# A hybrid attention block on Trainium2: the turned halves of a head are joined first in a period, its product moves between the second and the third projection quarter, and gates and norm rows are turned without TensorE

## The chip, the cores and the metric

The kernel runs on one core of one Trainium2 chip. Its time is the device time of one execution in microseconds (us); lower is better. The program has one instruction list for each engine: TensorE (PE in the profile, with weight loads as PEld), VectorE (DVE), ScalarE (ACT), GpSimd (POOL), and SyncE (SP), which here issues the DMA transfers. An engine works through its list in order, so an instruction that waits holds back everything listed behind it on that engine.

## The reference

One layer of a hybrid block for 512 tokens of width 2048, in float32. A combined projection gives queries, keys and values for eight "stick-breaking" heads (called sb below) and eight "forgetting" heads (called fox), each 128 wide, and eight forget gates.

```python
h = rmsnorm(x, g_attn[l])
proj = jnp.einsum('bsd,de->bse', h, w_in[l])
...
# sb head: strictly causal
log_beta = jax.nn.log_sigmoid(z)
log_keep = jnp.where(causal, jax.nn.log_sigmoid(-z), 0.0)
rest = lax.cumsum(log_keep, axis=3, reverse=True) - log_keep
a = jnp.where(causal, jnp.exp(log_beta + rest), 0.0)      # o = a @ v
# fox head: causal softmax with a bias from the summed log gates
z = z + c[:, :, i * Q_BLOCK:end, None] - c[:, :, None, :end]
p = jax.nn.softmax(jnp.where(causal, z, -jnp.inf), axis=-1)   # o = p @ v
...
x = x + jnp.einsum('bse,ed->bsd', mixed, w_out[l])   # mixed: each head's o, normalised
u = jax.nn.relu(jnp.einsum('bsd,df->bsf', rmsnorm(x, g_mlp[l]), w_up[l]))
x = x + jnp.einsum('bsf,fd->bsd', u * u, w_down[l])
```

The result is `rmsnorm(x, g_final)`.

## The kernel before

Every product is made with operands split into a high and a low part, both in a 32-bit format that TensorE reads in one pass; three matmuls (high by high, high by low, low by high) stand for one. The split of a weight tile costs ACT a cast (`cast`, tile `wh`) and DVE a subtraction (`low`, tile `wl`).

The program has stages: the first value projections, the projection of all other values with a seven-product scheme, the attention stage, and then the output, up and down projections, again with seven-product schemes. The change lies in the attention stage and just ahead of it.

The attention stage is cut into periods, numbered n = 0 to 16, each planned for 26.05 us (`TPER`). Jobs are entered with a planned time (`plan.at`), and the planned times only set the order in which instructions are recorded: each engine's list follows them, and no instruction waits for its planned time. In period n:

- PE projects the queries and keys of head n in four quarters (`project`, 24 matmuls each, tile `accq`): query first half, query second half, key first half, key second half. Between the first and the second quarter stand the scores of head n-1 (`scores`, tile `s`), and later the product of head n-2 with its values (`product`, tile `o`) and two matmuls that sum the squares of that product over the head (`norm_sums`, tile `ssq`).
- ACT and DVE turn the scores of head n-1 into weights in tile `w`. For a fox head these are `start`, `maxed`, `soft`, `scale`; for an sb head `start` (absolute value, ACT), `soft` (exponential and logarithm, ACT), `maxed` (DVE), `scan` (four running sums and a subtraction, DVE) and `weights` (exponential, ACT). Heads 0 to 7 of the order are fox, 8 to 15 sb, so scores are fox in n = 1 to 8 and sb from n = 9 on.
- The weights must be transposed. ACT copies them into two planes of 16-bit halves (`halves`, tile `pt`), a DMA transposes both planes (`turn_halves`), and in the next period ACT joins the halves again (`join_halves`, tile `pt`), casts the high part (`t_high`, tile `ph`), and DVE makes the low part (`t_low`, tile `pl`). `product` needs both.
- After the product, `square` (three ACT instructions), `square_low` (DVE; its result is what the second `norm_sums` matmul reads), `norm_1` (ACT) and `norm_2` (DVE) normalise the head.
- Beside this, the output weights are prepared by `WeightSums`: `high` and `low` split a part (tile `tboth`) that is stored to `wraws`, `sum` forms differences that are stored to `wsums`, `high_6` and `low_6` split one of these (tile `thi`) and store it to `whigh`. `tboth` and `thi` share one buffer, so each of these casts waits until the store of the one before has landed. In the fox periods the weights come in whole rows (`whole`, tile `mixed`): `high` stands once in every period and `high_6` in odd ones. Later they come in halves of a row (`half`, tile `ws`): in periods 8, 10, 12 and 14 stand both `high` and `high_6`, in periods 9, 11, 13 and 15 the `sum` steps alone.

Two more things belong to the change. The logs of the forget gates are summed with small matmuls into `cps` (`gates_3`), turned with four TensorE transposes (`gates_5`), and stored as `ckd` for the fox heads. And the row norms `r1`, which stand one per partition, are needed along the columns: `widen_r1` and `turn_r1` spread and turn them with four TensorE transposes into `trb`, and ACT copies them to `rb`, which `scale_u` multiplies into every query and key.

Up to period 2 the order of SP is the written one too; after it (`free_loads`) the tool that builds the program orders SP's transfers.

Of the kernel before, what the change touches and what calls it, by code (L numbers as in the profile page):

```python
# [8 lines left out]
F32 = mybir.dt.float32  # L9
# [6 lines left out]
P = 128  # L16
# [21 lines left out]
def block_kernel(ctx, tc, x, g_attn, w_in, b_f, g_out_sb, g_out_fox, w_out, g_mlp, w_up, w_down, g_final, y):  # L38
# [82 lines left out]
    vd = [dp.tile([P, TB, 2 * P], F32, name="vd0")] + [dp.tile([P, TB, 2 * NV], F32, name=f"vd{i}") for i in (1, 2)]  # L121
    ckd = dp.tile([NH, NT], F32, name="ckd")
    whigh = dp.tile([P, NH // 2, 2, NT], F32, name="whigh")

# [92 lines left out]
    with ExitStack() as stage:  # L217
# [352 lines left out]
        def gates_0():  # L570
            t_ = vf.tile([P, K8 * 2 * P], F32, tag="e3", name="gt")
            gate["tri"], gate["one"] = t_[:, :P], t_[:, P:2 * P]
            r_ = vf.tile([P, K8 * 2 * P], F32R, tag="e4", name="gr")
            gate["utri"] = r_[:, :P]
            gate["lf"] = r_[:, P:P + TB * 2 * NH].rearrange("p (t n) -> p t n", t=TB)
            gate["fe"] = t_[:, 4 * P:4 * P + TB * NH].rearrange("p (t n) -> p t n", t=TB)
            gate["ckT"] = t_[:NH, 5 * P:5 * P + NT]
# [19 lines left out]
        def gates_3():  # L597
            ps = gate["ps"] = accs[0].tile([P, NT], F32, tag="acc", name="cps")
            cps = gate["cps"] = ps[:, :TB * 2 * NH].rearrange("p (t n) -> p t n", t=TB)
            for t in range(TB):  # L600
                for i in range(t + 1):
                    pe.matmul(cps[:, t, :], gate["utri"] if i == t else onesr, gate["lf"][:, i, :], start=(t == 0 and i == 0),
                              stop=(i == t), skip_group_check=True)

# [4 lines left out]
        def gates_5():  # L609
            for t in range(TB):  # L610
                pe.transpose(gate["ps"][:NH, t * P:(t + 1) * P], cq[:, t, :], ident)
# [94 lines left out]
    with tc.tile_pool(name="att", bufs=1, side="right", reuse_waits="tile") as at, \  # L706
# [15 lines left out]

        def widen_r1():
            w = now["rw"] = at.tile([P, NT], F32, tag="uh4", name="rw")
            for t in range(TB):
                dve.tensor_copy(w[:, t * P:(t + 1) * P], r1[:, t:t + 1].to_broadcast([P, P]))

        def turn_r1():
            now["rb"] = atp.tile([P, NT], F32, tag="o", name="trb")
            for t in range(TB):  # L730
                pe.transpose(now["rb"][:, t * P:(t + 1) * P], now["rw"][:, t * P:(t + 1) * P], ident)

# [54 lines left out]
        class Head:  # L787
# [13 lines left out]
            def plan_sb(self, plan, t):  # L801
# [24 lines left out]
                last_ = self.i == 2 * NH - 1  # L826
                for dt, f in zip((6.4, 7.7, 10.2, 14.5, 19.2) if last_ else (7.4, 8.7, 11.25, 16.45, 21.1), (start, soft, maxed, scan, weights)):
                    plan.at(t + dt, f)

            def plan_fox(self, plan, t):  # L830
# [27 lines left out]

                for dt, f in zip((-4.0, 7.4, 12.2, 15.5, 17.8), (load, start, maxed, soft, scale)):
                    plan.at(t + dt, f)  # L860
# [13 lines left out]
            def turn_halves(self):  # L874
                self.two = wide("ph")
                sp.dma_start_transpose(self.two.bitcast(U16).rearrange("p (b t) -> p b t", t=P), self.one.bitcast(U16))
# [114 lines left out]
        def whole(m, t):  # L991
            w = WeightSums(m, (0, 1), lambda: mixed[:, :NH].rearrange("p (q a) n -> p q (a n)", a=2))
            e, o = (t, t + TPER) if m else (TPER, TPER)
            loads = (-4.0 if m == 1 else -15.0, 2.7) if m else (20.5, 20.6)
            highs, lows_, sums_, sixth = ((e + 3.0, o + 3.0), (e + 4.75, o + 4.75), (e + 5.5, e + 16.4, o + 5.5, o + 16.4), (o + 10.2, o + 20.2)) if m else \
                ((e + 4.3, e + 10.0), (e + 4.75, e + 10.9), (e + 5.5, e + 14.9, e + 19.6, e + 20.9), (e + 21.5, e + 23.3))
            for i in range(2):
                plan.at(t + loads[i], w.load, (i,))
                plan.at(highs[i], w.high, i)
                plan.at(lows_[i], w.low, i)  # L1000
            for i in range(4):
                plan.at(sums_[i], w.sum, i)
            plan.at(sums_[1] + 0.1, lambda: w.store(0, 2))
            plan.at(sixth[0], w.high_6)
            plan.at(sixth[1], w.low_6)
            plan.at(sixth[1] + 0.1, lambda: w.store(2, 4))

        def half(m, d, n):
# [8 lines left out]
            if d == 0:  # L1017
                jobs = [(8.3 if n == 7 else 13.0, load if n == 7 else w.load)]
                a = (3.0, 4.75, 5.5, 6.2, 6.9, 10.2, 16.4, 17.1, 20.8, 22.9) if n == 7 else (4.85, 6.2, 8.3, 9.0, 9.7, 11.15, 12.75, 13.45, 16.6, 23.2)
                jobs += [(TPER + dt, f) for dt, f in zip(a, (lambda: w.high(0), lambda: w.low(0), lambda: w.sum(0), lambda: w.sum(1), lambda: w.sum(2),  # L1020
                                                             lambda: w.high(1), lambda: w.low(1), lambda: w.sum(3), w.high_6, w.low_6))]
                jobs += [(TPER + a[-1] + 0.1, w.store)]
            else:
                jobs = [(TPER + 3.0, w.load)]
                jobs += [(TPER + dt, lambda j=j: w.sum(j)) for j, dt in enumerate((9.5, 10.2, 12.75, 13.45))] + [(TPER + 13.55, w.store)]
            for dt, f in jobs:
# [23 lines left out]
        for n in range(2 * NH + 1):  # L1050
            t = TPER * n
            i_s, i_o = n - 1, n - 2
            if n < 2 * NH:
                pieces = []
                for a, (which, hf) in enumerate(((0, 0), (0, 1), (1, 0), (1, 1))):
# [9 lines left out]
                    else:  # L1065
                        cast, low = ((-8.15, -4.45), (2.0, 3.5), (5.6, 9.4), (9.0, 10.6))[a] if n <= NH else ((-11.15, -3.55), (2.0, 3.5), (3.7, 4.9), (6.0, 7.1))[a]
                        if a == 0 and n == NH + 1:
                            cast, low = -8.15, -4.45
# [6 lines left out]
                late = n <= NH  # L1075
                for which, times in ((0, (19.0, 19.75, 20.45) if n == 0 else (14.2, 14.95, 19.5) if late else (14.2, 16.0, 21.8)),
                                     (1, (TPER + 0.3, TPER + 1.05, TPER + 2.6))):
                    for dt, f in zip(times, (scale_u, high_u, low_u)):
                        plan.at(t + dt, f, n, which)
            else:  # L1080
                pieces = []
                for a in range(4):
                    c = v_columns(order[2 * NH - 2])
                    k0 = 4 * a
                    w = Piece(w_in[k0 * P:(k0 + 4) * P, c:c + 2 * P].rearrange("(a p) c -> p a c", p=P), 4, 2 * P)
                    cast, low = ((-11.15, -3.55), (2.0, 3.5), (3.7, 4.9), (10.25, 11.7))[a]
                    pieces.append(w.plan(plan, t + (-21.0, -15.0, -14.0, -2.0)[a], t + cast, t + low))
# [8 lines left out]
            if 0 <= i_s < 2 * NH:  # L1096
# [4 lines left out]
                if n < 2 * NH:  # L1101
                    plan.at(t + (25.2 if sb else 23.8), H.halves)
                    plan.at(t + 26.2, H.turn_halves)
                else:
# [4 lines left out]
                if i_s % 2 == 0 and i_s < 2 * NH - 2:  # L1109
                    p_ = i_s // 2  # L1110
                    plan.at(t - 12.0 if p_ else t + 3.0, load_v, p_)
                    plan.at(t + (4.85 if sb else 6.7 if p_ else 12.0), high_v, p_)
                    plan.at(t + (8.3 if sb else 23.0 if p_ else 16.4), low_v, p_)
            if 0 <= i_o < 2 * NH - 1:
                H = heads[i_o]
                last_ = i_o == 2 * NH - 2
                for dt, f in zip((11.25, 13.6, 19.3) if last_ else (11.2, 13.7, 14.9), (H.join_halves, H.t_high, H.t_low)):
                    plan.at(t + dt, f)
                if last_:
                    continue  # L1120
                plan.at(t + 16.5, H.product)
                plan.at(t + 18.5, H.square)
                plan.at(t + 21.1, H.square_low)
                plan.at(t + 22.3, H.norm_sums)
                plan.at(t + 22.5, H.norm_1)
                plan.at(t + (24.4 if n > NH else 23.9), H.norm_2)
        for i, dt in ((2 * NH - 2, 1.0), (2 * NH - 1, 3.0)):
# [6 lines left out]
            plan.at(t_end + dt + 6.3, H.norm_2)  # L1134
        for dt, f in ((16.25, widen_r1), (17.0, turn_r1), (17.5, lambda: act.copy(rb, now["rb"]))):
            plan.at(dt, f)
        for m in range(4):
# [970 lines left out]
```

## Time and profile before

| | us |
|---|---|
| median of 3 runs | 2030.81 (2030.69 to 2032.73) |
| the profiled execution's own time | 2030.32 |
| its span, first to last instruction | 2028.6 |
| PE busy | 2004.1 (99%) |
| DVE busy | 1740.5 (86%) |
| ACT busy | 1204.0 (59%) |

The profiled execution's time is its span and 1.7 us around it. PE is busy in nearly all of the span, and a granted clock of 0.998 stands for the whole. Rows of the timeline give the start in us from the span's start, the duration, the engine, the line, the operation and the tiles; in brackets stands the idle time of that engine before the row and what ended it. Period n of the attention stage begins 5.45 us ahead of its scores, since a quarter of the projection takes that long.

### The profile page before, as it was taken

Reading aid. Unit: us, or ns where it says so; the run is one execution under the profiler, and the core shown is the slowest. Engines: PE = TensorE matmul, PEld = TensorE weight load, DVE = VectorE, ACT = ScalarE, POOL = GpSimd, SP = SyncE. Lnnn points to the kernel's source line nnn. Section 1 sums busy time; section 2 is a strip of 40 time slices with the busy share of each in tenths; the row PEclk is TensorE's granted clock in tenths of the full one; section 3 lists DMA queues with packets and bytes.
Section 4 is the critical chain, followed back from the end, with each engine's and each line's share of the span. In section 5 each row is a group of like instructions: output and inputs, shape, how many; then the busy total and the mean of one; then the engine's idle time right before and its main releaser. Section 6 shows DMA issues by size and latency. Waiting matters only on the chain.

```text
span 2028.6 us, 27079 instructions
## 1 busy us (share of the span) xinstructions
PE 2004.1 (99%) x10316; PEld 1733.7 (85%) x10316; DVE 1740.5 (86%) x1971; ACT 1204.0 (59%) x1645; POOL 60.3 (3%) x72
## 2 busy tenths in 40 slices
PE   9999999999999999999999999999999999999998
PEld 9998888877788889988888888888888888888887
DVE  7876787777778588899999999998799888888896
ACT  7544666777775556666767677676544343444444
POOL 0000000001010000000000000000000000000003
PEclk9999999999999999999999999999999999999999
DMA  7418877766667982576666666667785674674642
GB/s 261 154 63 263 263 221 214 225 186 194 182 211 261 298 272 86 161 242 188 208 210 184 217 202 195 208 194 252 249 299 198 224 261 166 233 259 170 223 159 89
DMA packets 309074, 423.28 MB, mean 209 GB/s; under 512 B 49176, under 2 KB 204872, under 8 KB 302416
## 3 DMA queue, kind: packets, MB, share of 16 engines
q1 hardware_dynamic: 308192, 419.44, 63.6%
q10 hardware_dynamic: 752, 2.11, 0.3%
q8 instruction: 81, 1.33, 0.3%
q14 instruction: 49, 0.40, 0.1%
HBM read 315.19 MB, written 96.49 MB: 203 GB/s over the span
## 4 chain that ended last, share of the span: by engine, by line
PE 79%; ACT 4%; DVE 3%; DMA 3%; issue 1%; ACTq 0%; SPq 0%; DVEq 0%
PE psa L1280 11%; PE accd L79 8%; PE accd L78 8%; PE accd L77 8%; PE psa L1278 6%; PE psc L1280 5%; PE psc L1278 3%; PE psb L1280 3%; PE accq L77 2%; PE accq L78 2%; PE accq L79 2%; DMA wraws<-tboth 2%; ACT pt L880 2%; PE psb L1278 1%; PE m L78 1%; PE m L79 1%
## 5 line engine op out<-in xcount | busy, mean ns | idle before, releaser
L1916 ACT CAST wh<-wd 128x1024 fp32r<-128x1024 f32 x126 | 125.0, 999 | 169.9 <-PE accd L79 59.3
L1802 DVE TENSOR_TENSOR wl<-wu,wh 128x1024 fp32r<-128x1024 f32 x158 | 192.6, 1219 | 12.1 <-ACT wh L1796 12.0
L77 PE MATMUL accq<-hH,wh 128*128 128x512 f32 x512 | 200.8, 392 | 0.0
L79 PE MATMUL accq<-hH,wl 128*128 128x512 f32 x512 | 199.8, 390 | 0.0
L78 PE MATMUL accq<-hL,wh 128*128 128x512 f32 x512 | 199.8, 390 | 0.0
L1796 ACT CAST wh<-wu 128x1024 fp32r<-128x1024 f32 x158 | 167.5, 1060 | 44.6 <-issue 28.2
L1280 PE MATMUL psa<-f,wh 128*128 128x512 f32 x720 | 179.1, 391 | 0.0
L79 PE MATMUL accd<-wh,uf 128*128 128x512 f32 x436 | 169.8, 389 | 0.0
L78 PE MATMUL accd<-wl,uf 128*128 128x512 f32 x436 | 169.7, 389 | 0.0
L77 PE MATMUL accd<-wh,uf 128*128 128x512 f32 x436 | 169.6, 389 | 0.0
L1280 PEld LDWEIGHTS psa<-f,wh 128*128 128x128 f32 x720 | 132.4, 188 | 25.5
L1923 DVE TENSOR_TENSOR wl<-wd,wh 128x1024 fp32r<-128x1024 f32 x126 | 143.8, 1150 | 10.6 <-ACT wh L1916 10.6
L1916 ACT CAST wx<-wd 128x1024 fp32r<-128x1024 f32 (+1 forms) x82 | 80.8, 994 | 105.8 <-PE accd L79 39.8
L1637 DVE TENSOR_TENSOR m<-m,accd 128x1024 f32<-128x1024 f32 x84 | 102.1, 1215 | 46.0 <-PE accd L79 46.0
L79 PEld LDWEIGHTS accq<-hH,wl 128*128 128x128 f32 x512 | 96.3, 188 | 20.3
L78 PEld LDWEIGHTS accq<-hL,wh 128*128 128x128 f32 x512 | 96.4, 188 | 19.1
L77 PEld LDWEIGHTS accq<-hH,wh 128*128 128x128 f32 x512 | 96.5, 189 | 18.9
L79 PE MATMUL accd<-wx,uf 128*128 128x512 f32 x284 | 110.6, 389 | 0.0
L78 PE MATMUL accd<-wx,uf 128*128 128x512 f32 x284 | 110.6, 389 | 0.0
L77 PE MATMUL accd<-wx,uf 128*128 128x512 f32 x284 | 110.6, 389 | 0.0
L1278 PEld LDWEIGHTS psa<-f,wl 128*128 128x128 f32 x720 | 96.0, 191 | 5.3
L1278 PE MATMUL psa<-f,wl 128*128 128x256 f32 x720 | 98.3, 283 | 0.0
(446 smaller groups left out, 5131.3 us busy)
## 6 DMA issues: line engine op xcount, KB each, us to landing
wu<-in_w_up_dram SPq DMA_DIRECT2D x60, 1024.0 KB, 6.6
ufd<-st SPq DMA_DIRECT2D x98, 512.0 KB, 4.2
wd<-in_w_down_dram SPq DMA_DIRECT2D x48, 1024.0 KB, 8.7
uf<-ufd SPq DMA_DIRECT2D x42, 1024.0 KB, 7.0
wraw<-in_w_in_dram SPq DMA_DIRECT2D x68, 512.0 KB, 5.6
wo<-wsums SPq DMA_DIRECT2D x28, 512.0 KB, 5.0
q<-in_w_in_dram SPq DMA_DIRECT2D x32, 384.0 KB, 6.0
wd<-in_w_down_dram SPq DMA_DIRECT2D x16, 768.0 KB, 6.9
```

Of the source, the lines that this page charges most:

```text
L77: pe.matmul(out, sh, mh, start=first, stop=False, skip_group_check=True)
L78: pe.matmul(out, sh, ml, start=False, stop=False, skip_group_check=True)
L79: return pe.matmul(out, sl, mh, start=False, stop=last, skip_group_check=True)
L880: act.copy(mingled(self.pt), apart(self.two))
L1278: ins = pe.matmul(ps[:, 2 * P:], lo[:, a, :], f_parts(p, a)[0], start=False, stop=last, skip_group_check=True)
L1280: ins = pe.matmul(ps, hi[:, a, :], f_both(p, a), start=a == PAIRS[0] and p in (1, 5), stop=last, skip_group_check=True)
L1637: dve.tensor_tensor(M[p][:, :, db, :], M[p][:, :, db, :], ps, op=ALU.add)
L1796: act.copy(rooms[k][0], srcs[k])
L1802: lows[0] = dve.tensor_tensor(lo, srcs.pop(k), hi.bitcast(F32), op=ALU.subtract)
L1916: act.copy(rooms[k + 3][0], srcs[k + 3])
L1923: dve.tensor_tensor(rooms[k + 2][1], srcs.pop(k + 2), rooms[k + 2][0].bitcast(F32), op=ALU.subtract)
```

## The change

1. **Order within a period.** `project` runs the third quarter in one piece, the product stands between the second and the third quarter (planned at 12.85 us of the period, before at 16.5), and the fourth quarter is cut in two with the sums of squares between them (in the periods up to 8 they stand ahead of the fourth quarter). `join_halves`, `t_high` and `t_low` are planned at 5.4, 8.5 and 9.8 (before 11.2, 13.7 and 14.9); `halves` a little earlier than before. All casts, low parts, weight sums and norm steps get new planned times. The transposing DMA writes into the buffer of `pl` (before `ph`).
2. **Gates.** The ten small matmuls of `gates_3` become four with a repeated operand. The four TensorE transposes are replaced by one DVE transpose of 32x32 blocks over a tile that holds the summed gates and `r1`; eight small DMAs store the pieces to `ckd` and to the new `r1d`.
3. **Norm rows.** `widen_r1`, `turn_r1` and the copy are gone; one DMA loads `rb` from `r1d`, repeated over all partitions.

```diff
         def gates_3():
-            for t in range(TB):
-                for i in range(t + 1):
-                    pe.matmul(cps[:, t, :], gate["utri"] if i == t else onesr, gate["lf"][:, i, :], ...)
+            pe.matmul(ps[:, :TB * 2 * NH], gate["utri"], gate["lf"].rearrange("p t n -> p (t n)"), start=True, stop=False, skip_group_check=True)
+            for i in range(TB - 1):
+                pe.matmul(cps[:, i + 1:, :], onesr, gate["lf"][:, i:i + 1, :].to_broadcast([P, TB - 1 - i, 2 * NH]), start=False,
+                          stop=i == TB - 2, skip_group_check=True)
...
         def gates_5():
-            for t in range(TB):
-                pe.transpose(gate["ps"][:NH, t * P:(t + 1) * P], cq[:, t, :], ident)
+            both = gate["both"]
+            act.mul(both[:, :TB * NH].rearrange("p (n t) -> p t n", t=TB), cq, -1.0)
+            act.copy(both[:, TB * NH:TB * NH + TB], r1s[0])
+            dve.transpose(gate["turned"], both)
 
         def gates_6():
-            act.mul(gate["ckT"], gate["ps"][:NH, :], -1.0)
-            sp.dma_start(ckd, gate["ckT"])
+            for q in range(4):
+                rows = gate["turned"][32 * q:32 * (q + 1)]
+                sp.dma_start(ckd.rearrange("n (t c) -> (n t) c", c=P)[:, 32 * q:32 * (q + 1)], rows[:, :32])
+                sp.dma_start(r1d[:, 32 * q:32 * (q + 1)], rows[:TB, 32:])
...
+        def load_rb():
+            sp.dma_start(rb, r1d.rearrange("t p -> (t p)").unsqueeze(0).to_broadcast([P, NT]))
...
             def turn_halves(self):
-                self.two = wide("ph")
+                self.two = wide("pl")
...
-                jobs = [(8.3 if n == 7 else 13.0, load if n == 7 else w.load)]
+                jobs = [({7: 8.3, 9: 25.0}.get(n, 13.0), load if n == 7 else w.load)]
...
-                marks = [(0, 0, 8, 0.0), (1, 0, 8, 7.35), (2, 0, 5, 12.85), (2, 5, 8, 18.2), (3, 0, 3, 20.2), (3, 3, 8, 22.7)]
+                marks = [(0, 0, 8, 0.0), (1, 0, 8, 7.35), (2, 0, 8, 14.8), (3, 0, 4, 20.3), (3, 4, 8, 23.4)]
...
-                for dt, f in zip((11.25, 13.6, 19.3) if last_ else (11.2, 13.7, 14.9), (H.join_halves, H.t_high, H.t_low)):
+                for dt, f in zip((11.25, 13.6, 19.3) if last_ else (5.4, 8.5, 9.8), (H.join_halves, H.t_high, H.t_low)):
...
-                plan.at(t + 16.5, H.product)
-                plan.at(t + 18.5, H.square)
-                plan.at(t + 21.1, H.square_low)
-                plan.at(t + 22.3, H.norm_sums)
...
+                late = n > NH
+                for dt, f in zip((12.85, 15.0, 21.7, 23.0, 23.4, 24.8) if late else (12.85, 17.1, 19.2, 20.25, 20.7, 22.05),
+                                 (H.product, H.square, H.square_low, H.norm_sums, H.norm_1, H.norm_2)):
```

The first place of which the prediction speaks is ACT's list in period 10, the first period in which an sb head's scores and both weight splits come together. Here `tboth` is the split of output weights, `w` an sb head's scores on their way to weights, `pt<-ph` (after the change `pt<-pl`) the join, `thi` the sixth part. Before:

```order
L968 CAST tboth_3945<-ws_3808 128x512
L169 CAST wh_3963<-wraw_3897 128x1024
L806 ACTIVATE w_3993<-s_3950 128x1280
L809 ACTIVATE w_3993<-w_3993 128x1280
L810 ACTIVATE w_3993<-w_3993 128x1280
L968 CAST tboth_4002<-ws_3808 128x512
L880 COPY pt_4004<-ph_3930 128x2x1280
L884 CAST ph_4030<-pt_4004 128x1280
L169 CAST wh_4038<-wraw_3948 128x1024
```

After the change the same stretch of ACT's list reads:

```order
L967 CAST tboth_3936<-ws_3895 128x512
L879 COPY pt_3941<-pl_3889 128x2x1280
L883 CAST ph_3985<-pt_3941 128x1280
L967 CAST tboth_3988<-ws_3895 128x512
L805 ACTIVATE w_3990<-s_3943 128x1280
L808 ACTIVATE w_3990<-w_3990 128x1280
L809 ACTIVATE w_3990<-w_3990 128x1280
L170 CAST wh_4020<-wraw_3885 128x1024
L979 CAST thi_4028<-ws_3895 128x512
```

The join and its cast have moved from behind the second `tboth` to ahead of it, and the three activations on the scores have moved from ahead of the second `tboth` to behind it. Periods 12 and 14 read the same.

The second place is SP's list at the end of period 1, up to the first transposing DMA; `mixed` are output weights for period 2, and `whigh` is the store after which the buffer of `thi` and `tboth` is free. Before:

```order
L988 DMA wsums_86<-mixed_1749 128x4x512
L835 DMA cb_2034<-ckd_90 128x512
L755 DMA vr_2194<-vd1_88 128x4x256
L964 DMA mixed_1749<-in_w_out_dram 128x2048
L985 DMA whigh_91<-thi_2031 128x512
L988 DMA wsums_86<-mixed_1749 128x4x512
L162 DMA wraw_2057<-in_w_in_dram 128x8x128
L876 DMA_TRANSPOSE ph_2084<-pt_2055 128x20x128
```

After the change:

```order
L754 DMA vr_2189<-vd1_88 128x4x256
L987 DMA wsums_86<-mixed_1750 128x4x512
L834 DMA cb_2030<-ckd_90 128x512
L963 DMA mixed_1750<-in_w_out_dram 128x2048
L875 DMA_TRANSPOSE pl_2033<-pt_2026 128x20x128
L984 DMA whigh_92<-thi_2028 128x512
L163 DMA wraw_2049<-in_w_in_dram 128x8x128
L987 DMA wsums_86<-mixed_1750 128x4x512
```

The transposing DMA now stands ahead of the `whigh` store instead of three transfers behind it, and still behind the load of `mixed`.

More of the change, by code (lines that the diff above doesn't have):

```diff
@@ L122, in block_kernel @@
     ckd = dp.tile([NH, NT], F32, name="ckd")
+    r1d = dp.tile([TB, P], F32, name="r1d")
     whigh = dp.tile([P, NH // 2, 2, NT], F32, name="whigh")
@@ L576, in gates_0 @@
             gate["fe"] = t_[:, 4 * P:4 * P + TB * NH].rearrange("p (t n) -> p t n", t=TB)
-            gate["ckT"] = t_[:NH, 5 * P:5 * P + NT]
+            gate["both"], gate["turned"] = (t_[:, a * P:a * P + 64] for a in (5, 6))
+            pool.memset(gate["both"], 0.0)
             tri = gate["tri"]
@@ L721, in free_loads @@
             manuals[-1].__enter__()
[L723 to L731, printed above, removed]
+        def load_rb():
+            sp.dma_start(rb, r1d.rearrange("t p -> (t p)").unsqueeze(0).to_broadcast([P, NT]))
         def scale_u(i, which):
@@ L826, in plan_sb @@
                 last_ = self.i == 2 * NH - 1
-                for dt, f in zip((6.4, 7.7, 10.2, 14.5, 19.2) if last_ else (7.4, 8.7, 11.25, 16.45, 21.1), (start, soft, maxed, scan, weights)):
+                for dt, f in zip((6.4, 7.7, 10.2, 14.5, 19.2) if last_ else (9.8, 11.0, 13.6, 17.0, 21.7), (start, soft, maxed, scan, weights)):
                     plan.at(t + dt, f)
@@ L857, in scale @@
                         dve.tensor_scalar(r, r, self.l[:, i:i + 1], None, op0=ALU.mult)
-                for dt, f in zip((-4.0, 7.4, 12.2, 15.5, 17.8), (load, start, maxed, soft, scale)):
+                for dt, f in zip((-4.0, 7.5, 12.4, 14.8, 17.5), (load, start, maxed, soft, scale)):
                     plan.at(t + dt, f)
@@ L1023, in half @@
             else:
-                jobs = [(TPER + 3.0, w.load)]
-                jobs += [(TPER + dt, lambda j=j: w.sum(j)) for j, dt in enumerate((9.5, 10.2, 12.75, 13.45))] + [(TPER + 13.55, w.store)]
+                jobs = [(TPER + 3.0 if n == 8 else 20.5, w.load)]
+                a = (11.3, 12.0, 16.3, 23.6) if n == 8 else (6.95, 7.65, 8.35, 9.05)
+                jobs += [(TPER + dt, lambda j=j: w.sum(j)) for j, dt in enumerate(a)] + [(TPER + a[-1] + 0.1, w.store)]
             for dt, f in jobs:
@@ L1075, in block_kernel @@
                 late = n <= NH
-                for which, times in ((0, (19.0, 19.75, 20.45) if n == 0 else (14.2, 14.95, 19.5) if late else (14.2, 16.0, 21.8)),
-                                     (1, (TPER + 0.3, TPER + 1.05, TPER + 2.6))):
+                for which, times in ((0, (19.0, 19.75, 20.45) if n == 0 else (14.4, 18.9, 19.9) if late else (12.8, 17.9, 23.6)),
+                                     (1, (TPER + 1.0, TPER + 1.7, TPER + 2.4))):
                     for dt, f in zip(times, (scale_u, high_u, low_u)):
@@ L1134, in block_kernel @@
             plan.at(t_end + dt + 6.3, H.norm_2)
-        for dt, f in ((16.25, widen_r1), (17.0, turn_r1), (17.5, lambda: act.copy(rb, now["rb"]))):
-            plan.at(dt, f)
+        plan.at(0.2, load_rb)
         for m in range(4):
```

25 lines of the change are left out of this document (11 added, 14 removed).

## The prediction

> **What bounds the kernel now.** I read the page first, for who is busy.
>
> ```profile
> PE 2004.1 (99%) x10316; PEld 1733.7 (85%) x10316; DVE 1740.5 (86%) x1971; ACT 1204.0 (59%) x1645; POOL 60.3 (3%) x72
> ```
>
> PE is the bound and some 24 us of the span are not its work. Whose fault those are, the waits of PE say (total us, times, longest):
>
> ```profile
> PE o L78 <- DVE pl L887: 10.2, 11, 1.1
> PE o L77 <- ACT ph L884: 4.7, 3, 2.0
> ```
>
> Nearly all of it is the product's two operands, `pl` and `ph`, both in the attention stage. Then I looked at how long each period lasts: the first matmul of the scores of successive heads, from PE's timeline.
>
> ```profile
> 207.45 0.39 PE L77 MATMUL s<-uh 128*128 128x512 f32 x1
> ...
> 261.06 0.39 PE L77 MATMUL s<-uh 128*128 128x512 f32 x1
> 287.15 0.39 PE L77 MATMUL s<-uh 128*128 128x512 f32 x1
> ...
> 422.12 0.39 PE L77 MATMUL s<-uh 128*128 128x512 f32 x1
> 451.70 0.39 PE L77 MATMUL s<-uh 128*128 128x512 f32 x1
> 478.91 0.39 PE L77 MATMUL s<-uh 128*128 128x512 f32 x1
> 509.18 0.39 PE L77 MATMUL s<-uh 128*128 128x512 f32 x1
> 536.39 0.39 PE L77 MATMUL s<-uh 128*128 128x512 f32 x1
> 567.70 0.39 PE L77 MATMUL s<-uh 128*128 128x512 f32 x1
> ```
>
> Period 4 (261.06 to 287.15) takes 26.09 us, with nothing waited for; I take that as an undisturbed one. Periods 11 and 13 take 27.21, 1.12 more: a single wait for `pl`, under 1.1, and the start-up behind it. I take the other periods of that sort (3, 5, 7, 8, 9, 15) to be like them: these eight, with 10, 12 and 14, are the 11 waits of the first row. Periods 10, 12 and 14 take 29.58, 30.27 and 31.31: together 12.9 above 26.09. Eight single waits at 1.12 are 9.0, so the two sorts are nearly the whole loss, 22 us.
>
> Part of the 12.9 is not waiting. The windows that hold scores of periods 10, 12 and 14 (busy time of PE, PEld, DVE, ACT, POOL, then granted clock, DMA share and GB/s) show it:
>
> ```profile
> 419.00:446.00 27.00, 24.05 (x115) 19.98 (x114) 20.83 (x25) 19.98 (x21) 2.74 (x4) 1.00 0.51 143
> 476.00:503.00 27.00, 24.94 (x112) 20.87 (x111) 20.37 (x24) 19.20 (x20) 3.92 (x4) 0.94 0.53 149
> 533.00:562.00 29.00, 25.88 (x116) 21.77 (x115) 20.93 (x25) 20.12 (x21) 3.06 (x4) 0.94 0.49 138
> ```
>
> In the last two the granted clock is 0.94, which is 0.06 x 27 = 1.6 us of lost clock each.
>
> Why is `ph` late there? ACT's and DVE's rows of period 10, which begins at 422.12 - 5.45 = 416.67, and the longest DMA pieces of the chain of waits:
>
> ```profile
> 424.28 1.24 ACT L806 ACTIVATE w<-s 128x1280 f32<-128x1280 f32 x1 [1.12 <-PE s L79]
> 428.23 1.49 DVE L813 SCALAR_TENSOR_TENSOR w<-s,w 128x1280 f32<-128x1280 f32 x1 [1.76 <-ACT w L810]
> 429.90 0.62 ACT L968 CAST tboth<-ws 128x512 fp32r<-128x512 f32 x1 [1.76 <-DMA wraws<-tboth]
> 430.43 3.09 ACT L880 COPY pt<-ph 128x2560 uint16<-128x2560 uint16 x1
> 433.55 1.26 ACT L884 CAST ph<-pt 128x1280 fp32r<-128x1280 f32 x1
> 434.71 1.04 ACT L169 CAST wh<-wraw 128x1024 fp32r<-128x1024 f32 x1
> 434.84 1.49 DVE L887 TENSOR_TENSOR pl<-pt,ph 128x1280 fp32r<-128x1280 f32 x1 [2.27 <-ACT ph L884]
> 436.25 2.96 DVE L819 TENSOR_TENSOR_SCAN w<-w 128x128 f32<-128x128 f32 x4
> 440.65 0.68 DVE L933 TENSOR_TENSOR pl<-ph,pl 128x512 fp32r<-128x512 f32 x1
> 441.86 1.22 DVE L176 TENSOR_TENSOR wl<-wraw,wh 128x1024 fp32r<-128x1024 f32 x1
> ```
> ```profile
> 199.69 2.70 DMA whigh<-thi
> 423.03 6.77 DMA wraws<-tboth
> 479.81 5.89 DMA wraws<-tboth
> 537.29 6.95 DMA wraws<-tboth
> ```
>
> The store of the first `tboth` goes out at 423.03 and takes 6.8 us. The second `tboth` needs its buffer and starts at 429.90; the join stands behind that cast, though its operand has long been turned.
>
> **The join first (single waits).** In the fox periods the join now starts at about 4.1 and ends at 7.2, the cast `ph` (1.26) is done at 8.5 and `pl` (1.49) between 9.4 and 10.9. PE asks for the product at about 13: two quarters of 5.45 and 2.2 of scores. In odd sb periods the halves end about 1.1 into the period, and a transposing DMA lands about 4.2 after issue by the median row of its tile:
>
> ```profile
> DMA to landing us min/median/max: 4.1/4.2/10.2
> ```
>
> So the join runs 5.4 to 8.5, `ph` to 9.8, `pl` to 11.3 to 12.4: 0.7 us ahead of PE. All eight single waits go: **-9.0**. What is late next is `square_low`, needed at about 23 and ready by 22.1 to 23.1 in odd sb periods, a thin margin that I price at nothing; if it is not there, each of the four odd sb periods loses up to 1.
>
> **Period 2.** The second order listing of the change shows the transposing DMA ahead of the `whigh` store. SP's rows:
>
> ```profile
> 193.26 0.37 SPq L988 DMA_DIRECT2D wsums<-mixed  x1
> 199.25 0.35 SPq L964 DMA_DIRECT2D mixed<-in_w_out_dram  x1
> 307.21 0.34 SPq L964 DMA_DIRECT2D mixed<-in_w_out_dram  x1
> 310.15 3.64 SPq L876 DMA_TRANSPOSE ph<-pt  x1
> ```
>
> The `wsums` store follows the second `sum`, whose planned time goes from 14.9 to 19.2: 193.26 + 4.3 = 197.6. The load of `mixed` overwrites what it stores and follows it by 6.0, as in the rows: 203.6. From such a load to the end of a transposing DMA that stands behind it SP takes 310.15 + 3.64 - 307.21 = 6.6: 210.2. Only then can `whigh` go, landing 2.7 later by its row: about 212.8, which is 10.8 into period 2 (202.0). ACT's list has that period's `tboth` waiting for it, with the join behind: 0.5 for the cast, 1.0 for a weight cast, 3.1, 1.26 and 1.49 make 18.1, against 13.1: PE waits 5.0, and 0.6 for `square_low` behind. Today this period loses 0.4, so **+5.2**. What it costs if the store lands at once (a transposing DMA of only 2.4 on SP, load 3 us sooner): +1; if all goes 5 us later, as the longest landing of that tile, 10.2, allows: +10.
>
> **Even sb periods.** The join no longer waits, but the wait is not gone: by the first order listing the second `tboth` now stands ahead of the three activations on the scores. Its store goes out at 423.03 - 416.67 = 6.4, and 0.6 later now, since norm steps stand ahead: 7.0. It takes 5.9 to 7.0: the second `tboth` starts at about 13.5. Behind it, by the rows: its own 0.53, scores activations up to `maxed` 428.23 - 424.28 = 3.95, `maxed` 1.49, a low part 1.22, `low_6` 0.68, scan and subtraction 440.65 - 436.25 = 4.40, `square_low` 0.68. That sums to 12.95 and puts `square_low`'s end at 26.4. PE asks at about 23.2 (26.09 less half a quarter and the sums): it waits 3.2 each. In period 10 the load of `ws` is new at 25.0 of period 9 behind the transposing DMA; its first `tboth` is held to about 8.3, so the product waits 1.8 and the sums 2.2: 4.0. A slower clock follows such waits in two of three windows today; I take half of 1.6 in each, 2.4. Sum 3.2 + 3.2 + 4.0 + 2.4 = 12.8 against 12.9: **-0.1**. Its ends are the rivals below.
>
> That half is a choice: no wait of PE here exceeds 2.0, yet 0.94 stands in two windows and 1.00 in the third. [...]
>
> **Gates and norm rows.** PE's rows:
>
> ```profile
> 144.28 0.17 PE L602 MATMUL cps<-gr 128*128 128x16 f32 x1
> 145.31 0.42 PE L77 MATMUL vx<-wh,hH 128*128 128x384 f32 x1
> 149.56 0.60 PE L611 MATMUL cps<-ident,cq 128*8 128x128 f32 x4
> 149.91 0.42 PE L77 MATMUL vy<-wh,s 128*128 128x384 f32 x1
> 167.80 0.40 PE L79 MATMUL accq<-hH,wl 128*128 128x512 f32 x1
> 168.67 0.48 PE L77 MATMUL accq<-hH,wh 128*128 128x512 f32 x1
> ```
>
> Ten matmuls take 1.03; four take about 0.4: -0.63. The transposes hold the next matmul back by 0.35. The norm turns make two matmuls stand 0.87 apart where 5.45/24 = 0.23 is usual: -0.64. Together **-1.6**. The additions (two short ACT copies, one DVE transpose, nine small DMAs) lie where those engines are not asked for by PE: `rb` is wanted at about 169, and its load can go from 158. If it came late, PE would wait there once, up to 2 us.
>
> **Sum.** -9.0 + 5.2 - 0.1 - 1.6 = -5.5, on the profiled 2030.3: 2024.8. The median stands 0.5 above that execution: **2025.3**.
>
> **Rivals.**
>
> 1. *The new waits hardly come.* If the `wraws` stores land in 2.7, as the lone `whigh` one did, the second `tboth` starts at 9.8 and `square_low` ends at 22.7, ahead of 23.2; 12.9 goes, and period 2 costs 1.2. Sum -9.0 - 12.9 + 1.2 - 1.6 = -22.3: **2008.5**. Against it: three rows of 5.9 to 6.95 for the same store in the same periods. For it: `sum` and `low` steps have moved in every period, so other transfers share the queues with it. 0.22.
> 2. *Slower: the second `tboth` holds up the scores.* A store that meets the transposing DMA of the period can last like the longest transfer of that tile, 10.2. Then the second `tboth` starts at 17.2, `square_low` ends at 30.1 and PE waits 7.0, with 1.6 of clock: 8.6 x 3 = 25.8 against 12.9, so +12.9 for -0.1: **2038.3**. It decides for slower than today (past 0.2%) from a store of about 9 us on. Against: 10.2 is the longest of its kind, the median 4.2, and the three stores' rows end at 6.95. 0.13.
> 3. *The clock halves after every long wait.* Full 1.6 in three periods, and as much behind the 5.0 of period 2: +2.4 + 1.6, so **2029.3**, no change. For: 0.94 in two of three windows with shorter waits than I forecast. 0.13.
>
> **How the numbers follow.** A measurement of this kernel can tell about 0.2%, 4.1 us, from no change. My own forecast has 0.52; its range is 2018 to 2031 by period 2's ends (-4 to +5) and the stores' ends (5.9 to 6.95, three times 0.5 to each side), with the clock at nothing or in full. Below 2026.7 is faster: two thirds of the forecast, 0.35, and all of rival 1, 0.22, and 0.02 of rival 3: 0.59. Same, to 2034.9: the rest of the forecast, less 0.03 that adds a store of over 9 us in one period and four lost margins, and most of rival 3: 0.24. Slower: rival 2, those 0.03 and 0.01 of rival 3: 0.17. The range for 8 in 10 takes the forecast, rival 3, and a good half of each outer rival: 2007 to 2036.
>
> **What would show it.** Right: no wait of the product for `pl` in the odd periods and their length at 26.1 to 26.3; the wait for the product in period 2 about 5; PE waiting for `square_low` in 10, 12 and 14, released by the DMA of `wraws` through ACT. Wrong: `wraws` stores of under 4 us or over 9; a period 2 without a wait; a wait for `rb`; odd sb periods that still lose 1.

## The result, and the profile after

The changed kernel takes 2038.70 us (median of 11 runs, 2036.54 to 2044.01) against 2031.47 before (11 runs): a ratio of 1.0037 with an interval of 1.0027 to 1.0046. It is slower by 7.2 us, where 2025.3 was forecast, and it lies above the stated range. The profiled execution of the changed kernel took 2042.29, its span 2040.6; it is one of the longer ones, 3.6 above its median, so the sums by period below are about that much too large.

PE's waits after the change (total us, times, longest):

```profile
PE ssq L938 <- DVE pl L932: 9.5, 3, 3.2
PE o L77 <- ACT ph L883: 9.2, 4, 5.6
PE o L78 <- DVE pl L886: 5.5, 5, 1.1
```

The single waits for `pl` have fallen from 11 to 5, but `ph` has doubled and a wait that did not exist, of the sums of squares (`ssq`) for `square_low`'s result, is the largest. The first matmul of each head's scores shows where:

```profile
182.44 0.39 PE L77 MATMUL s<-uh 128*128 128x512 f32 x1
206.12 0.39 PE L77 MATMUL s<-uh 128*128 128x512 f32 x1
241.21 0.39 PE L77 MATMUL s<-uh 128*128 128x512 f32 x1
267.30 0.39 PE L77 MATMUL s<-uh 128*128 128x512 f32 x1
...
423.86 0.39 PE L77 MATMUL s<-uh 128*128 128x512 f32 x1
456.07 0.39 PE L77 MATMUL s<-uh 128*128 128x512 f32 x1
484.42 0.39 PE L77 MATMUL s<-uh 128*128 128x512 f32 x1
514.39 0.39 PE L77 MATMUL s<-uh 128*128 128x512 f32 x1
547.19 0.39 PE L77 MATMUL s<-uh 128*128 128x512 f32 x1
579.00 0.39 PE L77 MATMUL s<-uh 128*128 128x512 f32 x1
```

The differences, less 26.09, are in this table, for every kernel that ran (period 15 is set against 24.97, to 0.01 the shortest one seen; where nothing waits it is shorter than the rest). Each row is one profiled execution.

| excess in us | 2 | 3 to 9 | 10 | 11 | 12 | 13 | 14 | 15 |
|---|---|---|---|---|---|---|---|---|
| before | 0.4 | 5.5 | 3.5 | 1.1 | 4.2 | 1.1 | 5.2 | 1.1 |
| changed | 9.0 | 0.0 | 6.1 | 2.3 | 3.9 | 6.7 | 5.7 | 1.8 |
| e1 gates only | 6.3 | 5.4 | 4.9 | 1.1 | 5.3 | 1.1 | 4.8 | 1.1 |
| e2 ws load behind the turn | 8.0 | 0.2 | 5.9 | 0.4 | 5.6 | 0.0 | 5.6 | 0.0 |
| e3 e2, split behind scores | 8.5 | 0.0 | 6.2 | 1.8 | 0.3 | 2.0 | 0.3 | 1.8 |
| e4 mixed load behind the turn | 13.2 | 0.0 | 5.2 | 1.6 | 5.4 | 1.5 | 6.6 | 0.1 |
| e5 all together | 8.0 | 0.2 | 0.2 | 0.8 | 0.3 | 0.8 | 0.4 | 0.8 |
| e6 before, join first only | 4.8 | 14.2 | 0.0 | 2.0 | 0.7 | 3.1 | 1.8 | 4.1 |
| e7 period 2 alone | 5.6 | 0.0 | 6.8 | 0.9 | 7.1 | 0.5 | 5.6 | 2.0 |
| e8 e5, period 2 again | 6.9 | 0.9 | 0.4 | 0.8 | 0.2 | 0.8 | 0.3 | 0.9 |
| e9 e5, ws load ahead | 6.9 | 0.1 | 0.3 | 6.5 | 0.0 | 5.3 | 0.3 | 6.4 |
| e10 e5, split first | 4.6 | 0.0 | 5.6 | 0.0 | 5.7 | 0.0 | 4.0 | 0.2 |

Between the two profiles: period 2 +8.6, periods 3 to 9 -5.5, periods 10, 12 and 14 +2.8, periods 11, 13 and 15 +7.4, and the scores of period 1 begin 1.3 earlier (182.44 against 183.76). That is +12.0, the whole difference of the spans.

**Odd sb periods.** SP's, ACT's and PE's rows of period 13, which begins at 508.94, and then the window from its scores to the next:

```profile
508.16 1.22 SPq L963 DMA_DIRECT2D ws<-in_w_out_dram  x2
509.47 0.55 SPq L163 DMA_DIRECT2D wraw<-in_w_in_dram  x1
510.39 7.12 SPq L875 DMA_TRANSPOSE pl<-pt  x1
```
```profile
519.73 3.07 ACT L879 COPY pt<-pl 128x2560 uint16<-128x2560 uint16 x1 [4.87 <-DMA pl<-pt]
524.15 0.39 PE L77 MATMUL o<-ph,vh 128*128 128x256 f32 x1 [2.23 <-ACT ph L883]
525.67 0.58 PE L78 MATMUL o<-pl,vh 128*128 128x256 f32 x1 [1.14 <-DVE pl L886]
```
```profile
514.39:547.19 32.80, 29.43 (x127) 24.53 (x125) 22.21 (x26) 20.30 (x21) 3.06 (x4) 0.90 0.69 180
```

Two loads of `ws` (output weights) stand just ahead of the transposing DMA. It takes 7.1 on SP and lands 9.3 after its issue, so the join starts 10.8 into the period, where it used to be planned at 11.2 and is now needed at 5.4. Waits of 2.2 and 1.1 follow, and a granted clock of 0.90, which is 3.3 of 32.8. Before, the same DMA of that period found no transfer in the 4 us ahead of it:

```profile
504.94 2.54 SPq L876 DMA_TRANSPOSE ph<-pt  x1
```

**Period 2.** It now begins at 200.67.

```profile
203.29 0.34 SPq L963 DMA_DIRECT2D mixed<-in_w_out_dram  x1
203.75 6.37 SPq L875 DMA_TRANSPOSE pl<-pt  x1
210.22 0.52 SPq L984 DMA_DIRECT2D whigh<-thi  x1
```
```profile
213.44 0.62 ACT L967 CAST tboth<-mixed 128x512 fp32r<-128x512 f32 x1 [8.64 <-DMA whigh<-thi]
219.29 0.58 PE L77 MATMUL o<-ph,vh 128*128 128x256 f32 x1 [5.64 <-ACT ph L883]
220.82 0.58 PE L78 MATMUL o<-pl,vh 128*128 128x256 f32 x1 [0.95 <-DVE pl L886]
```

**Even sb periods.** ACT's second `tboth` of period 10, and PE's second sum of squares of period 12:

```profile
434.33 0.62 ACT L967 CAST tboth<-ws 128x512 fp32r<-128x512 f32 x1 [1.89 <-DMA wraws<-tboth]
434.86 1.24 ACT L805 ACTIVATE w<-s 128x1280 f32<-128x1280 f32 x1
```
```profile
505.85 0.50 PE L938 MATMUL ssq<-pl,onesr 128*128 128x512 f32 x1 [3.23 <-DVE pl L932]
```

The scores wait behind a split that waits for a store, and `square_low` arrives 3.2 late.

### The profile page after: what moved, and what is told of

Its sections match the earlier page's. It is cut to its first block, busy times and chain, and to the rows that moved or that the text cites. A ratio compares the mean times of both kernels' runs of the same rounds, so it can differ in the third digit from the quotient of the medians.

```text
span 2040.6 us, 27057 instructions
## 1 busy us (share of the span) xinstructions
PE 2006.4 (98%) x10302; PEld 1734.9 (85%) x10302; DVE 1741.2 (85%) x1968; ACT 1201.0 (59%) x1645; POOL 63.6 (3%) x73
## 4 chain that ended last, share of the span: by engine, by line
PE 89%; DVE 4%; DMA 3%; ACT 3%; issue 1%; SPq 0%; POOL 0%; ACTq 0%; DVEq 0%
PE psa L1277 11%; PE accd L79 8%; PE accd L78 8%; PE accd L77 8%; PE psa L1275 6%; PE psc L1277 5%; PE accq L77 3%; PE accq L79 3%; PE accq L78 3%; PE psc L1275 3%; PE psb L1277 3%; PE psb L1275 1%; PE m L78 1%; PE m L77 1%; PE m L79 1%; DMA wraws<-tboth 1%
## 5 line engine op out<-in xcount | busy, mean ns | idle before, releaser
L78 PEld LDWEIGHTS accq<-hL,wh 128*128 128x128 f32 x512 | 97.0, 189 | 19.5
```

The source lines that it names most:

```text
L78: pe.matmul(out, sh, ml, start=False, stop=False, skip_group_check=True)
```

## The experiments

The theory after the result: three independent queues, each with the join or the scores behind a transfer, make the loss: the transposing DMA behind `ws` loads in odd sb periods, the second `tboth` ahead of the scores in even ones, and the SP chain in period 2. The rivals were that the gates' small DMAs cost time, or that DVE's own work sets the waits.

**e1.** The kernel before, with edits 2 and 3 alone.

> The kernel before, with only the new gates and norm rows (edits 2 and 3); the order of the attention periods is the old one. My theory (the new order of the periods causes the whole slowdown; this part takes PE work away): the scores of period 1 begin 1.3 us earlier, as they did in the whole change (182.44 against 183.76), all periods as long as before, 1 to 2 us less in all, about 2030. Rival (the small DMAs and the load of rb cost something later): as long as before or longer, with a wait of PE for qf in periods 0 and 1.

2031.27 (2029.37 to 2036.66), ratio 0.9997 with 0.9988 to 1.0005: no change that can be told. The scores of period 1 do begin earlier (182.07, 1.7 sooner), and nothing waits for `qf`: the rival's wait did not come, though its time, as long as before, did. The 1 to 2 us of my theory do not show in the time either, for the periods are not as long as before. In the profiled run, the longest of its eleven, period 2 exceeds by 6.3: the transposing DMA of period 1 went out at 202.55 and landed at 214.3, 14.0 into a period that now begins sooner, against 10.6 before. What PE gains ahead of period 2 can be lost there, since SP's chain does not move with it.

**e2.** The changed kernel; SP issues the `ws` load behind the transposing DMA.

```diff
-                sp.dma_start_transpose(self.two...
+                last_turn[0] = sp.dma_start_transpose(self.two...
...
-                with tc.issue_after(lows[0].ins):
+                with tc.issue_after(lows[0].ins if n == 7 else last_turn[0].ins):
...
-                jobs = [(TPER + 3.0 if n == 8 else 20.5, w.load)]
-                a = (11.3, 12.0, 16.3, 23.6) if n == 8 else (6.95, 7.65, 8.35, 9.05)
+                jobs = [(TPER + 3.0, w.load) if n == 8 else (26.5, load)]
+                a = (11.3, 12.0, 16.3, 23.6) if n == 8 else (10.2, 10.9, 14.0, 14.7)
```

> The changed kernel, with the load of ws for odd periods queued on SP behind the transposing DMA of the period, and the weight sums behind the low part of the weights. My theory (in periods 11, 13 and 15 the ws load just ahead of the transposing DMA stretches it from 2.6 to 5 to 7 us on SP, and that makes ph late): the transposing DMAs of these periods take 2.6 to 3.1 on SP, the product's waits there go, periods 11, 13, 15 exceed 26.09 by under 0.5 each (2.3, 6.7 and 0.7 in the changed kernel's profile); 5 to 9 us less than the change. Rival (the wraw and vr loads stretch it as well, or the late sums become the wait): the periods stay over 27.

2033.50, ratio 1.0003 (0.9994 to 1.0012), about 7 less than the change against its own runs of before. Period 13's transposing DMA on SP, from the timeline:

```profile
506.96 2.52 SPq L875 DMA_TRANSPOSE pl<-pt  x1
```

Periods 11, 13 and 15 exceed by 0.4, 0.0 and 0.0, as the theory said (its 0.7 for period 15 of the change is against 26.09, the table's 1.8 against 24.97). The sums moved too in this run; e9 below moves the loads alone.

**e3.** e2 with the second split behind the scores in even sb periods.

```diff
-(4.3, 5.7, 6.4, 7.1, 7.8, 9.75, 11.3, 12.0, 14.7, 16.3)
+(4.3, 5.7, 6.4, 7.1, 7.8, 12.5, 13.7, 13.71, 18.0, 23.2)
```

> The kernel of e2, with the second split of output weights (tboth) behind the three score activations in even sb periods, its low part behind maxed, and the sixth part late. My theory (the second tboth waits for the wraws store and holds up the scores, so square_low is late): the waits of ssq, 3.0 to 3.2 each in periods 10, 12 and 14, fall below 0.5 in 12 and 14; in 10 the first tboth is held by the late load of ws, so the wait of the product stays and that of ssq falls by less (to about 2.5). 7 to 9 us less than e2. Rival (DVE's own work sets square_low there): the waits of ssq stay above 2.

2027.36, ratio 0.9971 (0.9960 to 0.9982). Periods 12 and 14 fall from 5.6 to 0.3: DVE's own work was not the limit. The waits:

```profile
PE o L77 <- ACT ph L883: 7.5, 2, 4.6
PE ssq L938 <- DVE pl L932: 3.3, 3, 1.1
```

The gain, 6 us, is a little under the 7 to 9 expected, since the later sixth part puts the `wsums` store 2.6 ahead of the transposing DMA of odd periods, which then takes 3.7 to 3.9 on SP; these periods give 1.8, 2.0 and 1.8 back. In e5, where the store goes out 4.6 ahead, the DMA takes 2.4 to 2.6 and the three exceed by 0.8 each.

**e4.** The changed kernel, the load of `mixed` behind the transposing DMA of period 1.

```diff
-            loads = (-4.0 if m == 1 else -15.0, 2.7) if m else (20.5, 20.6)
+            loads = (-1.9 if m == 1 else -15.0, 2.7) if m else (20.5, 20.6)
```

> The changed kernel, with the load of mixed for period 2 behind the transposing DMA of period 1 on SP. My theory (the transposing DMA was held up on SP by that load, which waits for the wsums store, and shares the queues with it): the transposing DMA goes out at about 200.2 instead of 203.8 and takes 2.6 on SP, whigh lands at 206 to 208, tboth of period 2 then waits for the load (209 to 211), and period 2 exceeds 26.09 by 2 to 4 instead of 9.0: 5 to 7 us less than the change. Rival (the wsums store and the wraw loads hold it up): period 2 stays at 7 to 9 over.

2039.49, ratio 1.0038 (1.0024 to 1.0052): nothing gained, and period 2 is worse, 13.2. SP and ACT:

```profile
200.04 5.62 SPq L875 DMA_TRANSPOSE pl<-pt  x1
...
207.62 0.46 SPq L963 DMA_DIRECT2D mixed<-in_w_out_dram  x1
```
```profile
216.59 0.62 ACT L967 CAST tboth<-mixed 128x512 fp32r<-128x512 f32 x1 [11.80 <-DMA mixed<-in_w_out_dram]
```

The transposing DMA went out at 200.04 as foretold, but took 5.6, not 2.6, behind a store and two loads of the last 4 us; and the load landed 8.9 after its issue. The loads traded places: my theory of this period was incomplete, its ACT half (the split ahead of the join) had not been touched.

**e5.** e3, the low of the sixth part at 21.9, the `ws` load of period 9 back at 13.0 with earlier sums, and in periods 1 and 2:

```diff
-((e + 3.3, o + 3.3), (e + 4.5, o + 4.5), (e + 6.4, ...
+((e + (9.0 if m == 1 else 3.3), o + 3.3), (e + (10.5 if m == 1 else 4.5), o + 4.5), (e + (11.2 if m == 1 else 6.4), ...
-(e + 6.4, e + 19.2, e + 20.6, e + 21.8)
+(e + 6.4, e + 14.9, e + 20.6, e + 21.8)
```

> The kernel of e3, and: in period 1 the second sum back at 14.9, in period 2 the split of output weights behind the join; the ws load of period 9 back at 13.0 with the sums of that period earlier; the sixth part's low ahead of a weight's low, so that the wsums store goes out earlier. My theory (period 2: 8.5, period 10: 6.2, periods 11, 13, 15: 4.5 above 26.09 in e3, all from waits for transfers that these edits take off ACT's path): period 2 exceeds by under 2, period 10 by under 1, the others by under 1 each; 10 to 16 us less than e3, 2012 to 2018. Rival (the transposing DMA of period 1 itself, 5.6 to 9.6 us on SP in every order so far, is the limit in period 2; and an early ws load is late in another period): period 2 keeps 4 to 6, less than 10 us gained.

2017.95, ratio 0.9929 (0.9915 to 0.9943): 14 less than before and at the upper end of the 2012 to 2018 expected, but 9.4 less than e3, not 10 to 16. All sb periods are within 1 of 26.09 (period 15 of 24.97). But period 2 keeps 8.0, more even than the rival's 4 to 6; whether by its cause, e8 asks. PE's waits are now

```profile
PE ssq L938 <- DVE pl L932: 4.1, 4, 2.6
PE o L78 <- DVE pl L886: 1.1, 1, 1.1
PE o L77 <- ACT ph L883: 0.4, 1, 0.4
```

**e6.** The kernel before, with the join alone moved.

```diff
-(11.2, 13.7, 14.9), (H.join_halves, H.t_high, H.t_low)
+(5.4, 8.5, 9.8), (H.join_halves, H.t_high, H.t_low)
```

> The kernel before, with only the join, its cast and the low part planned at 5.4, 8.5 and 9.8; product, norm steps, weight splits, loads and gates as before. My theory (the join's place is what the eight single waits and the waits of ph depend on): the waits of the product go in nearly all periods, 11 of them to at most 3; 10 to 18 us less than before. Rival (the join ahead of the scores makes the weights or square_low late, and PE waits there instead): waits of ssq or of the next product appear, gain under 5 us.

2037.99, ratio 1.0025 (1.0014 to 1.0035). The rival is right, and 6 us are lost where it said a small gain: every wait of the product is gone, and others stand in their place.

```profile
PE ssq L939 <- DVE pl L933: 10.2, 11, 2.4
PE accq L77 <- ACT wh L169: 4.1, 3, 1.9
PE ssq L938 <- ACT pl L930: 2.2, 3, 1.0
```

**e7.** The changed kernel with e5's two edits of periods 1 and 2 alone.

> The changed kernel, with the second sum of period 1 back at 14.9 and the split of output weights in period 2 behind the join and its cast; nothing else. My theory (the 9.0 us above 26.09 in period 2 are ACT's wait in tboth for whigh, or in e4 for the load of mixed, with the join queued behind): period 2 exceeds by under 2, 6 to 8 us less than the change, about 2031. Rival (the transposing DMA lands late whatever stands ahead of it): period 2 keeps 4 to 6.

2036.58, ratio 1.0023 (1.0014 to 1.0033), about 3 less than the change where 6 to 8 were expected. Period 2 falls from 9.0 to 5.6, the rival's figure, but not by the rival's cause alone: the product waits 0.5 and 1.1, and the sums of squares wait 1.0 and 1.8.

**e8.** e5 with the load of `mixed` at -1.9, and in period 2 the split at 14.6, its low part at 16.2 and the sums at 16.3 and 17.0.

> The kernel of e5, with the load of mixed for period 2 behind the transposing DMA of period 1, and that period's split of output weights behind three weight casts, its low part and sums behind the weights' low parts. My theory (in e5 period 2 still exceeds by 8.0 since the transposing DMA shares its queues with that load, 6.3 on SP, and the weight load behind it is late, so that DVE and square_low are): the transposing DMA takes 3 to 5 on SP, the weight loads behind it go 2 to 3 sooner, period 2 exceeds by under 4: 4 to 7 us less than e5. Rival (as in e4 the loads only trade places, the transposing DMA stays at 5 to 6): period 2 stays at 6 to 9.

2016.21, ratio 0.9920 (0.9906 to 0.9933), not to be told from e5: the 4 to 7 us did not come. The transposing DMA is as fast as anywhere, and the product does not wait; the sums of squares do (SP's row, then PE's):

```profile
201.89 2.64 SPq L875 DMA_TRANSPOSE pl<-pt  x1
```
```profile
222.04 0.50 PE L937 MATMUL ssq<-pl,onesr 128*128 128x512 f32 x1 [0.53 <-ACT pl L929]
225.59 0.80 PE L938 MATMUL ssq<-pl,onesr 128*128 128x512 f32 x1 [3.05 <-DVE pl L932]
```

So the transposing DMA is not what holds period 2 at 6.9 in e8, and e5, where it took 6.3, is about as long. DVE's row of e8 shows what stood ahead of `square_low` in its list:

```profile
222.32 1.23 DVE L975 TENSOR_TENSOR mixed<-mixed 128x1024 f32<-128x1024 f32 x1 [1.40 <-DMA mixed<-in_w_out_dram]
```

This is a weight sum (`sum`) that waited 1.40 (2.40 in e5) for the second load of `mixed` of the period, issued at 215.15; the last fox step `scale` and `square_low` stand behind it. It is again an operation held up by one that waits for a transfer. No run puts this sum behind `square_low`, so how much of period 2 it costs stays open.

**e9 and e10.** e5 with one thing undone each. In e9 the lists of ACT and DVE are those of e5, and only SP's order differs, as in this piece (e5 with -, e9 with +):

```order
-L875 DMA_TRANSPOSE pl<-pt 128x20x128
-L963 DMA ws<-in_w_out_dram 128x2x512 x2
+L963 DMA ws<-in_w_out_dram 128x2x512 x2
+L875 DMA_TRANSPOSE pl<-pt 128x20x128
```

> The kernel of e5 with one thing undone: the ws loads of periods 11, 13 and 15 stand ahead of the transposing DMA on SP again; the lists of ACT and DVE are those of e5, row for row. My theory: the transposing DMAs of these three periods go from 2.4 to 2.6 back to 5 to 7 on SP, PE waits for ph or pl there, and the three periods exceed 26.09 by 4 to 10 together more than in e5: the time is 3 to 9 us longer than e5. Rival (the place on SP does nothing; e2 gained by its later sums): as long as e5.

2032.49, ratio 0.9998 (0.9989 to 1.0007): 14.5 more than e5, for the place of the transposing DMA among two loads on SP in three periods. Period 13's, in e9 and then in e5:

```profile
502.33 1.22 SPq L963 DMA_DIRECT2D ws<-in_w_out_dram  x2
503.66 5.40 SPq L875 DMA_TRANSPOSE pl<-pt  x1
```
```profile
498.80 2.55 SPq L875 DMA_TRANSPOSE pl<-pt  x1
501.44 1.21 SPq L963 DMA_DIRECT2D ws<-in_w_out_dram  x2
```

Periods 11, 13 and 15 take 6.5, 5.3 and 6.4 instead of 0.8 each. My theory had the cause, but not the size (3 to 9).

> The kernel of e5 with another thing undone: the second split of output weights ahead of the scores in periods 10, 12 and 14, with its low part and the sixth part, planned as in the changed kernel. My theory: PE waits 3.0 to 3.3 for square_low in each of the three, with 1.6 of clock behind some of them, so 9 to 14 us longer than e5. Rival (those waits were shadowed by the late ws load of period 10 or the product's wait): under 5 us longer.

2030.21, ratio 0.9987 (0.9978 to 0.9996): 12.3 more than e5, within the 9 to 14 expected; in the profiles periods 10, 12 and 14 take 14.3 more than in e5. That execution is the shortest of its eleven, 3.7 below the median: period 2 and the odd sb periods were 5.6 shorter in it than in e5.

```profile
PE ssq L938 <- DVE pl L932: 11.4, 4, 3.2
```

## Why the prediction was wrong, point by point

- **Single waits, -9.0: wrong, and the main error.** In periods 3 to 9 they went, -5.5. In periods 11, 13 and 15 they did not: their excess rose from 3.4 to 10.8 in the profile, where I had booked nothing left; that is 10.8 of the 17.5 between the -5.5 forecast and the +12.0 of the profiles. The step that failed is "a transposing DMA lands about 4.2 after issue by the median row". These DMAs went out near where 1.1 into the period was worked out (1.4, 1.5, and 0.15 ahead of period 15), but by the new order all three stand behind two `ws` loads: they take 5.1 to 7.1 on SP and land 7.3, 9.3 and 8.5 after issue. The move was in the diff (`TPER + 3.0 ... 20.5, w.load`), and the price was in the rows that I had quoted: 3.64 on SP behind a load of `mixed`, and a longest landing of 10.2. I priced every move on ACT and DVE there, and none on SP. e2 and e9 show the cause. Its size in one profile varies: 10.8 in the change, 3.2 and 3.4 in e4 and e7 with the same SP lists there. In e7 the DMA of period 13 took 6.0 as well, but went out 1.3 ahead of the period, where it went out 1.5 into it in the change, for PE had lost 3.2 more in period 12 (7.1 against 3.9): what one period loses can hide the next one's wait.
- **Period 2, +5.2: right in its mechanism, too small.** `whigh` went out at 210.22 where 210.2 was worked out, to the tenth by luck: the load of `mixed` followed the `wsums` store 1.5 sooner than I took it to, and the store itself went out 1.2 later. The period itself began 1.3 sooner, for the PE work removed ahead of it, so the same landing was later in it: a wait of 5.6 and 0.95, and 2.4 more behind them, at a granted clock of 0.90 over the period, which I had not priced: +8.6. The 0.6 for `square_low` did not come in this period.
- **Even sb periods, -0.1: the waits right, what stands around them not.** `square_low` was 3.0, 3.2 and 3.2 late, as worked out (3.2), and by the steps worked out: in period 12 the second `tboth` began 13.7 into the period where 13.5 was forecast. But the three exceed by 15.7 together, not 12.8. In period 10 product and sums waited 5.2, not 4.0 (1.1 twice and 3.0), and behind the waits each period lost another 0.6 to 0.9 that no term of the sum held. The clock took less than the 2.4 booked: it was granted at 1.00, 1.00 and 0.95, which is 1.6 of the third period. In e2, e4 and e7, where the three exceed by 17.1 to 19.5, it took about 3, 5 and 6.5 by the same windows (0.95 twice; 0.95 and 0.90; 0.95, 0.90 and 0.95). This term varies from run to run (the granted clock of the change's eleven runs goes from 0.992 to 0.995), so that the 2.4 booked came near it is luck.
- **Gates and norm rows, -1.6: right in place** (-1.3 at the scores of period 1), but e1 shows that it brings no time that can be told as long as period 2 gives it back.
- **The rivals.** Rival 2 had nearly the time, 2038.3, by a mechanism that did not come: the `wraws` store of period 10 went out at 428.87 and the second `tboth` began at 434.33, 5.5 later (6.6 and 6.9 in periods 12 and 14), where that rival needs 9 or more. That its time fits is luck. Rival 1, stores landing in 2.7, did not come either. Rival 3 was partly true: the clock fell to 0.50 behind the waits of period 2 (for 6.8 us) and of one of the three even sb periods (for 3.4).

The two queues of the sb periods are most of the loss: with both undone the same change is 14 us faster than the kernel before (e5), and either of them alone costs 14.5 or 12.3 of that (e9, e10). They do not add: together that would be 27, but the change is some 21 above e5. The third, in period 2, was not undone by any run: it keeps 8.0 in e5 and 6.9 in e8.

## What to carry to other kernels

When an operation is moved earlier, work out again when its operand lands, and read SP's list ahead of that transfer: slack that nobody needed before (here the 5.8 us by which the join moved towards the transposing DMA) is the first thing spent. Here it paid to put a transfer that something waits for ahead of bulk loads (e9, without it, took 14.5 us more), and a cast that waits for a store behind the work that does not (e10, without it, 12.3 more). Test an order by undoing one part in the good version (e9, e10), where no other wait hides it: the same part looked worth 7 us in the changed kernel and 14 in e5.

## What was not expected of the hardware

- In these profiles a transposing DMA took 2.4 to 2.8 us on SP with no transfer issued in the 3 us ahead (3.05 once, with a `wsums` store 3.55 ahead), 3.6 to 4.1 with a `wsums` store 1.8 to 3.3 us ahead, and 4.4 to 7.1 with two `ws` loads 0.7 to 3.7 us ahead (in the change, e4 and e7 a weight load besides); what SP had to issue next went out behind it (in period 13 of the change at 517.63, where the DMA had gone out at 510.39 and took 7.12).
- PE ran slower behind some short waits and not behind a longer one. Behind the 2.23 and 1.14 of period 13 its matmuls of the next quarter took 0.63 and came 0.43 apart, but behind the 3.23 of period 12 they took 0.40 and came 0.23 apart, as ever. Narrow windows of the profile show where the granted clock changes: it is 0.50 from 524.90 to 531.72, two stretches of 3.41, and 1.00 on either side. The other stretches at 0.50 of the attention stage, 217.70 to 224.52 and 569.27 to 572.68, begin 90 steps of 3.413 ahead of 524.90 and 13 behind it; the two of the kernel before, 492.82 to 496.23 and 550.85 to 554.26, begin 17 such steps apart. With the windows laid in steps of 3.41 from 524.90, the waits fall like this, period 12's in the first two rows (PE's busy time stands first, the clock third from the end):

```profile
501.01:504.42 3.41, 1.61 (x8) 0.98 (x6) 3.38 (x5) 0.45 (x1) 0.00 (x0) 1.00 0.91 238
504.42:507.83 3.41, 1.99 (x9) 1.64 (x10) 3.32 (x4) 2.48 (x3) 1.20 (x2) 1.00 0.58 225
521.49:524.90 3.41, 0.81 (x3) 0.19 (x2) 0.78 (x1) 3.38 (x3) 0.00 (x0) 1.00 1.08 366
524.90:528.31 3.41, 2.64 (x11) 2.64 (x12) 1.69 (x3) 3.35 (x4) 0.00 (x0) 0.50 0.33 93
```

The wait of 3.23 is split between two windows, in each of which PE is busy for about half, and the clock stays. The two shorter waits leave PE 0.81 of one window, and the next has half the clock. That fits the 0.94 of the kernel before, too: there PE was busy for 1.35 of 489.41 to 492.82, and the clock was 0.50 in the 3.41 behind. So in these rows it is where a wait falls, as well as how long it is, that makes it dear.
